# Second mixer: a head's two decay projections by seven block products, with token sums, weight sums and remainders on GpSimd

## The chip, the cores and the metric

The kernel runs on one core of one Trainium2 chip. The metric is the device time of one execution in microseconds (us); less is better. Engines are named as the profile names them: PE is TensorE, with PEld for its weight loads, DVE is VectorE, ACT is ScalarE, POOL is GpSimd and SP is SyncE, which issues most of the transfers.

## What is computed

Two layers of a diffusion backbone over 512 latent tokens with a prefix of 256 context tokens, model width 1024, all in float32. Layer 0 is a mixer of gated linear attention beside grouped-query attention and then a feed-forward block; layer 1 is an HGRN2 mixer and a feed-forward block. The change touches layer 1's mixer alone. What that computes, cut to the parts that matter:

```python
q, f_fwd, f_bwd, i, og = split(h @ w_in)          # h: 768 tokens x 1024, eight heads of 128 columns each
q = silu(q)
for d, f in enumerate((f_fwd, f_bwd)):            # the two decay projections of a head
    log_f = logaddexp(log(lb[d]), log1p(-lb[d]) + log_sigmoid(f))
    k = -expm1(log_f)                             # that is (1 - lb) * (1 - sigmoid(f))
    o[d] = scan(q, k, i, log_f)                   # context first, from a zero state; then the latent tokens
out = rms(o[0] + o[1]) * gain * silu(og)          # latent tokens alone
```

The decay projections are needed for all 768 tokens, the query projection and the gate og for the 512 latent ones.

## The kernel before

A float32 product is made of three matmuls. Each operand is split into H, a copy in the format that TensorE multiplies at speed, and L = x - H, the remainder; the product is H·H + H·L + L·H (`mm3`, and `product` in the change). A weight block goes through `fetched` (L793): a transfer into a `raw` buffer of 128x1024 (three of them), a cast to `wH` on ACT (L803) and a subtraction into `wL` on DVE (L804); there are four `wH` and four `wL` buffers. The activations of the mixer, `h`, lie split in four tiles `x0` to `x3`: H and L of its first four row blocks of 128, and H and L of its last four, each over 768 tokens.

The feed-forward blocks already make their 256-column products in seven block products in place of eight (`seven`, L900, with the table `SEVEN` at L59): the 1024 rows are cut into two halves, the columns into two blocks of 128, the tokens into two halves of 384. Sums of token halves (T1 to T4) are multiplied with sums of weight blocks (U1, U2, S4, V), and DVE and ACT put the results together.

The second mixer, `odd_mixer` (L1400), goes through the heads in a software pipeline. `prep` makes a head's projections: for each direction d a 128-column block of weights against 256 context and 512 latent tokens (`gemm_T`, tile `ff`, L1414 to L1418), a sigmoid (L1419), the gates `f`, `fc`, `kc`, `arr` (L1423 to L1426), the running product over the context (L1431, L1436) and `kc` times it (L1439); then the query projection (`fq`, L1444) with q = silu, two products q·f and the sum `ks` (L1446 to L1450). After the `yield` it transposes `kc` (`kcT`) and makes the first states (`S0`). `scan` (L947) then runs on the head before: seven levels, each with two copies on ACT (L1012), two products arr·f in place on DVE (L1017) and one f·f (L1018); block matrices (`pch`, `pbh`), transposes (`knph`), states (`pdh`, L1084) and outputs (`poh`), whose rms needs a power on POOL (`rstd`, L686). The order of these pieces on PE is written out by the `go(...)` lines at the end of `odd_mixer`, and held to by `pinned`: PE's instructions run in the order of the text. The other engines' instructions are ordered by the framework's scheduler, and each engine runs its queue in order.

Ahead of the mixer the projection i of the scan is made (`values`, L2124, tile `nat`), while DVE adds up the modulation vectors of layer 1 (`mod_late`, L573, tile `macc`, L613 and L615); a few matmuls on those sums (`mod_acc`) stand among PE's `nat` matmuls, in the written order. Behind the mixer's heads come the gate products (`gate`, tile `nat`) and the output projection.

PSUM has eight banks: two double ones (`mm`), two `sc`, two `tr`. The `hg` pool holds the mixer's tiles and takes the place of pools that the feed-forward block has released; a tile waits for the last use of what lay there.

Of the kernel before, what the change touches and what calls it, by code (L numbers as in the profile page):

```python
# [8 lines left out]
F32 = mybir.dt.float32  # L9
F32R = mybir.dt.float32r  # L10
# [306 lines left out]
class Net:  # L317
# [24 lines left out]
    def banks(self, narrow):  # L342
        if self.ps is not None:
            self.ps.release()
        self.narrow = narrow
        self.ps = self.tc.alloc_tile_pool(name={True: "psn", False: "psw", None: "pso"}[narrow], bufs=1, space=PSUM, reuse_waits="tile")
# [21 lines left out]
    def sc_tile(self, name, which=None):  # L368
        if which is None:
            self.side = which = 1 - self.side  # L370
        return self.ps.tile([P, 512], F32, tag=f"sc{which}", bufs=1, name=name)

# [574 lines left out]
    def scan(self, pool, nm, arr, q, ksum, dscale, f, nt, hpp, V, first, ends, o_evac):  # L947
# [54 lines left out]
        while b < P:  # L1002
            qk = pool.tile([P, 2, N], F32, tag=f"qk{N}", bufs=4 if N > CTX else 3, name=f"qk{nm}{b}")
            qks[b] = qk

            blk = arr.rearrange("p a (n h o) -> p a n h o", h=2, o=b)
            qkv = qk.rearrange("p a (n h o) -> p a n h o", h=2, o=b)
            nb = N // (2 * b)
            tv = f[:, :, : 2 * nb].rearrange("p a (n h) -> p a n h", h=2)
            for lo, half in ((0, 0), (2, 1)):  # L1010
                dst = blk[:, lo : lo + 2, :, half, :]
                nc.scalar.copy(qkv[:, :, :, half, :], dst)  # L1012
                tb = tv[:, :, :, 1 - half]
                if lo == 2:
                    tb = tb[:, ::-1, :]
                tb = tb[:, :, :, None].to_broadcast([P, 2, nb, b])
                nc.vector.tensor_tensor(dst, dst, tb, op=ALU.mult)  # L1017
            nc.vector.tensor_tensor(f[:, :, :nb], tv[:, :, :, 0], tv[:, :, :, 1], op=ALU.mult)  # L1018
# [49 lines left out]
        for d, (order, steps) in enumerate(orders):  # L1068
# [10 lines left out]
            for i, t in enumerate(steps):  # L1079
                S = pool.tile([P, P], F32, tag="S", bufs=8 if hpp > 1 else 10, name=f"S{nm}{d}{t}")  # L1080
# [318 lines left out]

    def odd_mixer(self, h, fi):  # L1400
        nc, I = self.nc, self.I
        w = I["odd_w_in"][0]
        with self.pool("hg") as gp:
            ones = gp.tile([P, CTX], F32, tag="ones", name="ones")
            nc.gpsimd.memset(ones, 1.0)
            def prep(hd, given):
# [3 lines left out]
                ks = gp.tile([P, SEQ], F32, tag="ks", bufs=2, name=f"ks{hd}")  # L1410
                S0, kcs = [], []
                for d in range(2):
                    pt = self.mm_tile(f"ff{hd}{d}")
                    W = self.unit_cols(w, (1 + d) * D + hd * P)  # L1414
                    self.gemm_T(pt, W, h, ((512, 256),))
                    yield
                    self.gemm_T(pt, W, h, ((0, 512),))
                    sg = gp.tile([P, NT], F32, tag="sg", bufs=2, name="sg")  # L1418
                    nc.scalar.activation(sg, pt[:, :NT], AF.Sigmoid)  # L1419
                    lb, lb1, nlb1 = (x[:, d, hd : hd + 1] for x in (self.lb, self.lb1, self.nlb1))  # L1420
                    fc = gp.tile([P, CTX + 32], F32, tag="fc", bufs=2, name="fc")
                    kc = gp.tile([P, CTX], F32, tag="kc", bufs=2, name="kc")
                    nc.vector.tensor_scalar(fc[:, :CTX], sg[:, SEQ:], lb1, lb, op0=ALU.mult, op1=ALU.add)  # L1423
                    nc.scalar.activation(kc, sg[:, SEQ:], AF.Identity, bias=lb1, scale=nlb1)
                    nc.vector.tensor_scalar(f[:, d, :], sg[:, :SEQ], lb1, lb, op0=ALU.mult, op1=ALU.add)
                    nc.scalar.activation(arr[:, 2 * d, :], sg[:, :SEQ], AF.Identity, bias=lb1, scale=nlb1)  # L1426

                    pr = gp.tile([P, CTX], F32, tag="pr", bufs=1, name="pr")
                    if d == 0:
                        nc.vector.memset(pr[:, CTX - 1 : CTX], 1.0)  # L1430
                        nc.vector.tensor_tensor_scan(  # L1431
                            pr[:, 0 : CTX - 1][:, ::-1], fc[:, 1:CTX][:, ::-1], ones[:, 1:CTX], 1.0, op0=ALU.mult, op1=ALU.mult
                        )
                    else:
                        nc.vector.memset(pr[:, 0:1], 1.0)
                        nc.vector.tensor_tensor_scan(  # L1436
                            pr[:, 1:CTX], fc[:, 0 : CTX - 1], ones[:, 1:CTX], 1.0, op0=ALU.mult, op1=ALU.mult
                        )
                    nc.vector.tensor_tensor(kc, kc, pr, op=ALU.mult)  # L1439

                    kcs.append(kc)
                    yield
                pq = self.mm_tile(f"fq{hd}")
                self.gemm_T(pq, self.unit_cols(w, hd * P), h, ((0, 512),))  # L1444
                q = gp.tile([P, SEQ], F32, tag="q", bufs=2, name=f"q{hd}")
                nc.scalar.activation(q, pq[:, :SEQ], AF.Sigmoid)  # L1446
                nc.vector.tensor_tensor(q, q, pq[:, :SEQ], op=ALU.mult)
                nc.vector.tensor_tensor(arr[:, 1, :], q, f[:, 1, :], op=ALU.mult)
                nc.vector.tensor_tensor(arr[:, 3, :], q, f[:, 0, :], op=ALU.mult)
                nc.vector.tensor_tensor(ks, arr[:, 0, :], arr[:, 2, :], op=ALU.add)  # L1450
# [3 lines left out]
                for kc in kcs:  # L1454
                    pk = self.tr_tile("kcT")
                    for i in range(2):
                        self.tr(pk[:, i * P : (i + 1) * P], kc[:, i * P : (i + 1) * P], self.ident)
                    kn = gp.tile([P, CTX], F32, tag="kcn", bufs=2, name="kcn")
                    nc.scalar.copy(kn, pk[:, :CTX])
                    kns.append(kn)  # L1460
# [16 lines left out]
            def head(hd, arr, q, ks, f, S0):  # L1477
# [3 lines left out]
                def evac(hh, t0, n, po):  # L1481
                    o = fi[:, 0:LT, hd * P : (hd + 1) * P]
                    nc.scalar.copy(o, po)
                    sq = gp.tile([P, LT, P], F32, tag="sq", bufs=1, name="sq")
                    nc.scalar.activation(sq, po, AF.Square)
                    ss = self.sm.tile([P, LT], F32, tag="ss4", name="ss4")
                    nc.vector.tensor_reduce(ss, sq, axis=AX.X, op=ALU.add)
# [3 lines left out]
                return self.scan(gp, f"h{hd}", arr, q, ks, 1.0, f, LT, 1, V, S0, None, evac)  # L1491

            def gate(c0, early):
                us = self.wide_units(4 * D + c0)
                for t0 in (0, 2):
# [6 lines left out]
                    for a in range(2):  # L1502
                        pt = self.mm_tile("nat")[:, :512]
# [14 lines left out]
            for hd in range(8):  # L1518
# [4 lines left out]
                go(new, new)  # L1523
# [17 lines left out]

        cat = Split(h.pool)
# [742 lines left out]
```

## Time and profile before

| | before |
|---|---|
| median of 3 runs | 1674.42 us (1673.77 to 1677.1) |
| the profiled execution | 1675.78 us, its span 1674.0 us |
| TensorE clock granted, mean | 0.998 |
| DVE busy, whole span | 1311.1 us, 78% |
| ACT busy, whole span | 916.1 us, 55% |
| POOL busy, whole span | 129.4 us, 8% |
| the eight heads' projections on PE | from 982.0 to 1221.1 us |

A row of a group gives line, engine, operation, output<-inputs, the shape and the count; then the busy time in us and the mean of one in ns; then how long the engine was idle just before, and what ended that. A row of the timeline gives start and duration in us. A row of the chain gives start, duration and what ran. A row of the windows gives the stretch, its length and the busy time of PE, PEld, DVE, ACT and POOL with the number of instructions. A row of merged instructions (x2, x3) spans from the first start to the last end.

### The profile page before, as it was taken

The page shows a single profiled execution, that of the slowest core. Times are in us where ns is not written, and L with a number is a line of the kernel's source. Part 1 is how long each engine was busy: PE and PEld are TensorE (multiplying, and loading weights), DVE is VectorE, ACT ScalarE, POOL GpSimd, SP SyncE. Part 2 cuts the span into 40 slices and gives each one's busy share as a digit, 9 for nine tenths or more (in the row PEclk, how much of TensorE's full clock was granted, in tenths as well). Part 3 has the DMA queues.
Part 4 walks back from the last instruction along what each step waited for, and adds up shares of the span by engine and source line. Part 5 has one row for each costly group of instructions (what it writes and reads, how often), then busy time and mean ns, then how long its engine had stood idle before and what let it go on. Part 6 is the DMA issues. An engine that isn't in the chain of part 4 may idle for free.

```text
span 1674.0 us, 32524 instructions
## 1 busy us (share of the span) xinstructions
PE 1644.8 (98%) x13407; PEld 1481.1 (88%) x13407; DVE 1311.1 (78%) x2097; ACT 916.1 (55%) x1551; POOL 129.4 (8%) x139
## 2 busy tenths in 40 slices
PE   9999999999999999999999999999999999999998
PEld 7899987888999999998887888888888899999886
DVE  5999678976898988777668648788775599987887
ACT  5745567845544443446447436666664565555664
POOL 2004110011000000002102000000000100000310
PEclk9999999999999999999999999999999999999999
DMA  9641012164243445249525541121124333333973
GB/s 336 213 132 41 3 45 86 50 227 160 80 126 114 139 151 176 78 153 205 100 84 193 200 127 57 48 65 40 51 65 150 126 114 115 114 101 102 226 164 138
DMA packets 184736, 204.79 MB, mean 122 GB/s; under 512 B 7142, under 2 KB 141836, under 8 KB 184588
## 3 DMA queue, kind: packets, MB, share of 16 engines
q1 hardware_dynamic: 173996, 181.98, 34.7%
q0 software_dynamic: 9024, 17.30, 5.9%
q10 hardware_dynamic: 1568, 3.43, 0.6%
q8 instruction: 105, 1.72, 0.4%
q14 instruction: 43, 0.35, 0.1%
HBM read 193.23 MB, written 9.46 MB: 121 GB/s over the span
## 4 chain that ended last, share of the span: by engine, by line
PE 83%; DVE 8%; ACT 3%; DMA 3%; issue 2%; POOL 0%; SPq 0%; DVEq 0%; ACTq 0%; POOLq 0%
PE nat L355 12%; PE a L355 10%; PE ff L355 8%; PE E L355 7%; PE oproj L355 6%; PE x L355 6%; PE o L355 5%; PE D L355 4%; PE b L355 3%; PE fq L355 3%; PE gqk L355 2%; PE pearly L355 2%; PE q L355 2%; PE S L355 2%; PE poh L355 1%
## 5 line engine op out<-in xcount | busy, mean ns | idle before, releaser
L355 PE MATMUL nat<-wH,x 128*128 128x256 f32 (+2 forms) x968 | 226.7, 322 | 1.2 <-ACT x L2014 0.6
L860 ACT CAST wH<-raw 128x1024 fp32r<-128x1024 f32 x120 | 124.8, 1051 | 102.7 <-DVE raw L885 40.7
L355 PEld LDWEIGHTS nat<-wH,x 128*128 128x128 f32 x968 | 161.9, 190 | 19.5 <-ACT natq L1196 1.7
L861 DVE TENSOR_TENSOR wL<-raw,wH 128x1024 fp32r<-128x1024 f32 x120 | 145.7, 1222 | 23.6 <-ACT wH L860 23.3
L355 PE MATMUL nat<-wL,x 128*128 128x256 f32 (+2 forms) x484 | 153.5, 317 | 1.8 <-DVE wL L804 1.8
L804 DVE TENSOR_TENSOR wL<-raw,wH 128x1024 fp32r<-128x1024 f32 x79 | 95.8, 1222 | 50.6 <-ACT wH L803 49.8
L355 PE MATMUL ff<-x,wH 128*128 128x512 f32 (+1 forms) x512 | 127.6, 340 | 0.0
L686 POOL TENSOR_TENSOR rs<-ms,neghalf 128x1 f32<-128x1 f32 (+2 forms) x56 | 60.1, 1076 | 777.7 <-DVE ms L684 777.6
L803 ACT CAST wH<-raw 128x1024 fp32r<-128x1024 f32 x79 | 82.2, 1050 | 68.5 <-PE ff L355 19.7
L355 PE MATMUL oproj<-wH,x 128*128 128x512 f32 x320 | 102.2, 394 | 0.4 <-ACT x L1330 0.4
L355 PEld LDWEIGHTS nat<-wL,x 128*128 128x128 f32 x484 | 92.1, 190 | 7.8 <-DVE wL L804 2.7
L615 DVE SCALAR_TENSOR_TENSOR macc<-mraw,scT,macc 128x1024 f32<-128x1024 f32 x70 | 88.0, 1282 | 11.6 <-DMA mraw<-in_mod_w_dram 11.4
L355 PEld LDWEIGHTS ff<-x,wH 128*128 128x128 f32 x512 | 87.3, 190 | 10.0
L355 PE MATMUL x<-wH,two 128*128 128x512 f32 x280 | 90.5, 392 | 0.9 <-DVE y L1851 0.7
L1773 POOL DMA_DIRECT2D t<-in_ffn_w_down_dram x36 | 41.9, 1200 | 640.1 <-DVE t L1812 338.3
L1012 ACT COPY qkh<-arr 128x512 f32<-128x512 f32 x112 | 70.2, 641 | 36.6 <-DVE arr L1017 32.3
L355 PE MATMUL ff<-x,wL 128*128 128x256 f32 (+1 forms) x256 | 86.2, 337 | 0.0
L885 DVE TENSOR_TENSOR raw<-raw 128x512 f32<-128x512 f32 x120 | 82.8, 690 | 2.8
L1017 DVE TENSOR_TENSOR arr<-arr,f 128x512 f32<-128x512 f32 x112 | 74.4, 688 | 2.0 <-ACT qkh L1012 0.3
L355 PEld LDWEIGHTS oproj<-wH,x 128*128 128x128 f32 x320 | 59.9, 188 | 13.0 <-ACT x L1330 1.0
L355 PE MATMUL a<-T,wH 128*128 128x384 f32 (+1 forms) x320 | 70.5, 309 | 0.6 <-ACT qb L923 0.5
L355 PE MATMUL E<-T,wH 128*128 128x384 f32 (+1 forms) x320 | 70.4, 309 | 0.7 <-DVE go L938 0.7
(425 smaller groups left out, 4558.6 us busy)
## 6 DMA issues: line engine op xcount, KB each, us to landing
mraw<-in_mod_w_dram SPq DMA_DIRECT2D x80, 512.0 KB, 4.4
raw<-in_ffn_w_gate_dram SPq DMA_DIRECT2D x44, 512.0 KB, 3.9
raw<-in_ffn_w_up_dram SPq DMA_DIRECT2D x44, 512.0 KB, 4.9
raw<-in_odd_w_in_dram SPq DMA_DIRECT2D x40, 512.0 KB, 3.7
t<-in_ffn_w_down_dram POOLq DMA_DIRECT2D x30, 512.0 KB, 8.3
raw<-in_ffn_w_down_dram SPq DMA_DIRECT2D x28, 512.0 KB, 8.0
mraw<-in_mod_w_dram SPq DMA_DIRECT2D x32, 256.0 KB, 6.3
raw<-in_even_w_in_dram SPq DMA_DIRECT2D x16, 512.0 KB, 5.9
```

The costliest lines, as they stand in the source:

```text
L355: return self.pin(self.nc.tensor.matmul(*a, **k))
L615: nc.vector.scalar_tensor_tensor(a, u, w, a, op0=ALU.mult, op1=ALU.add)
L686: nc.gpsimd.tensor_tensor(rs, ms, self.neghalf.to_broadcast([P, w]), op=ALU.pow)
L803: self.casts = self.casts[-1:] + [nc.scalar.copy(H[:, :m], raw[:, :m])]
L804: vector.tensor_tensor(L[:, :m], raw[:, :m], H[:, :m].bitcast(F32), op=ALU.subtract)
L860: self.nc.scalar.copy(H, f)
L861: self.nc.vector.tensor_tensor(L, f, H.bitcast(F32), op=ALU.subtract)
L885: add = lambda o, x, y: nc.vector.tensor_tensor(o, x, y, op=ALU.add)
L1012: nc.scalar.copy(qkv[:, :, :, half, :], dst)
L1017: nc.vector.tensor_tensor(dst, dst, tb, op=ALU.mult)
L1773: add = lambda o, src: self.pin(nc.gpsimd.dma_start(out=o, in_=src, accum_op=ALU.add))
```

## The change

- **Products.** A head's two directions become the two column blocks of one product of 1024 rows, 256 columns and 768 tokens, cut as in `SEVEN`: 7 products of 4 row blocks x 3 matmuls with 384 columns, in the order 11, 22, U1, 12, U2, S4, V. Before there were 2 x 8 x 3 matmuls with 256 columns and as many with 512. ACT copies or negates four results out of PSUM, DVE adds four more; the sigmoid is taken in three pieces.
- **Token sums.** `half_sums`, traced ahead of the first head, makes T1, T2, T4 and T3 (128x1536 each, H and L, in a new pool `T` of 48 KB a partition): 13 two-input operations on POOL, with four casts on ACT and four subtractions on DVE. The sums are used by all eight heads.
- **Weights.** A head's two decay blocks come in two transfers as before (and a third for the query). POOL makes the sums in place (four additions of 128x512); each of nine operands of 128x512 gets its H from ACT and its remainder L from POOL, in a ring of four places cut out of two of the four `wH` and `wL` buffers. The other two become four places for the scan's levels (`qk`), which lose their own tiles.
- **Smaller moves.** `ks` is added on POOL; `q` and `ks` lie in an `mraw` buffer; the running product is made in place, without `fc`, `pr` and `ones`; the squares of the outputs stay in PSUM, where DVE sums them; the S ring has 8 places in place of 10.
- **PSUM.** Four single banks `p0` to `p3` take the place of the two double ones in the mixer; A and D change banks from head to head.
- **Order.** `prep` has six steps in place of seven: products 11 and 22; U1, 12 and U2; S4 and V; the query; the transposes; the first states. One `go(new, new)` becomes `go(new)`.
- **Gate.** The first gate block's weights go into the places of T1, T2, T4 and T3.

```diff
+    def half_sums(self, h, pool, temp):
...
+        a, b = (temp().rearrange("p a n -> p (a n)")[:, : 4 * n].rearrange("p (k n) -> p k n", k=4) for _ in range(2))
+        op = lambda o, x, y, f: nc.gpsimd.tensor_tensor(o, x, y, op=f)
...
+            if sign > 0:
+                nc.scalar.copy(H, x)
+                nc.vector.tensor_tensor(L, x, H.bitcast(F32), op=ALU.subtract)
...
+        def less(x, y):
+            op(a, f32[x][0], f32[y][0], ALU.subtract)
+            op(b, f32[x][1], f32[y][1], ALU.subtract)
+            op(a, a, b, ALU.add)
+
+        less("11", "12")
+        split("T1", a)
+        for i in range(2):
+            op(b if not i else b, a if not i else b, f32["22"][i], ALU.add)
+        split("T2", b, -1.0)
+        for i in range(2):
+            op(a, b if not i else a, f32["21"][i], ALU.subtract)
+        split("T4", a)
+        less("22", "12")
+        split("T3", a)
...
+            def operand(x):
+
+                H, L = turned(ring)
+                nc.scalar.copy(H, x)
+                nc.gpsimd.tensor_tensor(L, x, H.bitcast(F32), op=ALU.subtract)
+                return [z.rearrange("p (k n) -> p k n", k=4) for z in (H, L)]
+
+            def weights(hd):
+                (w11, w12), (w21, w22) = (fetch((1 + d) * D + hd * P) for d in range(2))
+                add = lambda o, x, y: nc.gpsimd.tensor_tensor(o, x, y, op=ALU.add)
+                yield operand(w11)
+                yield operand(w22)
+                add(w22, w21, w22)
+                yield operand(w22)
+                yield operand(w12)
+                add(w21, w21, w11)
+                add(w11, w11, w22)
+                yield operand(w11)
+                add(w12, w12, w11)
+                yield operand(w12)
+                yield operand(w21)
+
+            def product(pt, W, X, start, stop):
+                for k in range(4):
+                    for i, (x, y) in enumerate(((0, 0), (0, 1), (1, 0))):
...
-                for d in range(2):
-                    pt = self.mm_tile(f"ff{hd}{d}")
-                    W = self.unit_cols(w, (1 + d) * D + hd * P)
-                    self.gemm_T(pt, W, h, ((512, 256),))
-                    yield
-                    self.gemm_T(pt, W, h, ((0, 512),))
...
+                    product(pt, next(W), forms[xn], new, True)
...
+                nc.gpsimd.tensor_tensor(ks, arr[:, 0, :], arr[:, 2, :], op=ALU.add)
...
-                nc.vector.tensor_tensor(ks, arr[:, 0, :], arr[:, 2, :], op=ALU.add)
...
                 go(outs, old)
-                go(new, new)
+                go(new)
                 go(outs, old, scan)
                 go(new, new)
                 go(scan, scan)
```

More of the change, by code (lines that the diff above doesn't have):

```diff
@@ L1402, in odd_mixer, with turned, fetch @@
         w = I["odd_w_in"][0]
+        n2 = NT // 2
+        tp = self.open_pool("T")
         with self.pool("hg") as gp:
[L1404 to L1405 removed]
+            self.banks(4)
+            own = {x: [self.wp.tile([P, WU], F32R if i < 2 else F32, tag=f"w{x}", bufs=4, name=f"w{x}") for i in range(4)] for x in "HL"}
+            ring = [[own[x][i // 2][:, 512 * (i % 2) : 512 * (i % 2) + 512] for x in "HL"] for i in range(4)]
+            levels = [own[x][i].rearrange("p (a n) -> p a n", a=2) for i in (2, 3) for x in "HL"]
+            forms = self.half_sums(h, tp, lambda: gp.tile([P, 4, SEQ], F32, tag="arr", bufs=2, name="Tsum"))
+            ones = self.one.to_broadcast([P, CTX - 1])
+            order = [SEVEN[i] for i in (0, 4, 1, 2, 3, 5, 6)]
+            def turned(xs):
+                x = xs.pop(0)
+                xs.append(x)
+                return x
+            def fetch(c0):
+                r = self.wp.tile([P, WU], F32, tag="raw", bufs=3, name="raw")
+                nc.sync.dma_start(out=r.rearrange("p (k n) -> p k n", k=KD), in_=w[:, c0 : c0 + P].rearrange("(k p) m -> p k m", p=P))
+                return [r[:, 512 * i : 512 * i + 512] for i in range(2)]
+            def operand(x):
[20 more added lines that the diff above has]
+                    for i, (x, y) in enumerate(((0, 0), (0, 1), (1, 0))):
+                        self.mm(
+                            pt, W[x][:, k, :], X[y][:, k, :], start=start and k == 0 and i == 0, stop=stop and k == 3 and i == 2,
+                            skip_group_check=True,
+                        )
```

134 lines of the change are left out of this document (90 added, 44 removed).

## The prediction

> **What bounds the kernel now.** I read the page's busy shares first, then the chain of work that ended last, then one head's stretch of it.
>
> ```profile
> PE 1644.8 (98%) x13407; PEld 1481.1 (88%) x13407; DVE 1311.1 (78%) x2097; ACT 916.1 (55%) x1551; POOL 129.4 (8%) x139
> ...
> PE 83%; DVE 8%; ACT 3%; DMA 3%; issue 2%; POOL 0%; SPq 0%; DVEq 0%; ACTq 0%; POOLq 0%
> ```
>
> PE is the bound overall. The change sits in layer 1's mixer, so that stage decides. The chain there, and the busy times of the stretch from one head's `ff` piece to the next head's:
>
> ```profile
> 448.52 2.08 PE E L355 x12
> ...
> 982.29 16.68 PE ff L355 x96
> ...
> 1081.27 5.68 PE ff L355 x24
> 1086.95 5.44 PE fq L355 x24
> ...
> 1094.97 2.88 PE ff L355 x24
> ...
> 1099.62 8.35 PE ff L355 x48
> ```
>
> ```profile
> 1081.27:1112.80 31.53, 31.53 (x400) 28.10 (x399) 25.12 (x57) 19.68 (x36) 1.44 (x1) 1.00 0.18 52
> ```
>
> A head takes 31.53 us, PE is busy in all of it, and the granted clock is full. DVE has 25.12 us of work, ACT 19.68, POOL 1.44. Only PE's work sets the pace; DVE has 6.4 us to spare.
>
> **PE's saving.** A head's `ff` pieces are 5.68 + 2.88 + 8.35 = 16.91 us. A block product of the new shape (12 matmuls of 384 columns) exists in the feed-forward block: 2.08 us. Seven make 14.56. So 2.35 us go per head and the head would take 29.18; the first head's piece (16.68) loses 2.1. Seven heads and the first: 7 x 2.35 + 2.1 = **-18.6 us**, if nothing else makes PE wait. All else of PE stays.
>
> **DVE per head.**
>
> ```profile
> L1017 DVE TENSOR_TENSOR arr<-arr,f 128x512 f32<-128x512 f32 x14 | 9.3, 687 | 0.1
> L804 DVE TENSOR_TENSOR wL<-raw,wH 128x1024 fp32r<-128x1024 f32 x3 | 3.7, 1225 | 1.7 <-ACT wH L803 1.7
> L1018 DVE TENSOR_TENSOR f<-f 128x32 f32<-128x32 f32 (+6 forms) x7 | 2.2, 307 | 0.1
> ...
> L1439 DVE TENSOR_TENSOR kc<-kc,pr 128x256 f32<-128x256 f32 x2 | 0.8, 422 | 0.1
> ...
> L1489 DVE TENSOR_TENSOR fi<-fi,rs 128x512 f32<-128x512 f32 x1 | 0.7, 692 | 0.9 <-POOL rs L686 0.9
> ...
> L1448 DVE TENSOR_TENSOR arr<-q,f 128x512 f32<-128x512 f32 x1 | 0.7, 686 | 0.0
> ...
> L1431 DVE TENSOR_TENSOR_SCAN pr<-fc,ones 128x255 f32<-128x255 f32 x1 | 0.7, 683 | 0.0
> ...
> L1450 DVE TENSOR_TENSOR ks<-arr 128x512 f32<-128x512 f32 x1 | 0.7, 665 | 0.0
> ```
>
> ```profile
> L931 DVE TENSOR_TENSOR go<-go,b 128x384 f32<-128x384 f32 x10 | 5.5, 551 | 0.5 <-PE b L355 0.3
> ```
>
> DVE loses the three remainders (3.7) and `ks` (0.7) and gains four additions out of PSUM of 0.55 (2.2): 25.1 - 4.4 + 2.2 = 22.9, with the two dropped memsets 22.8. Of that, operations with two inputs in SBUF are 9.3 + 2.2 + 0.8 + 0.7 + 2 x 0.7 (q·f) + 2 x 0.7 (running products) = 15.8 us, or 69%.
>
> **ACT per head.**
>
> ```profile
> L803 ACT CAST wH<-raw 128x1024 fp32r<-128x1024 f32 x3 | 3.1, 1048 | 3.0 <-PE fq L355 1.9 <-PE ff L355 1.1
> ```
>
> ```profile
> L860 ACT CAST dH<-ws 128x512 fp32r<-128x512 f32 x40 | 24.9, 621 | 28.1 <-PE a L355 17.4 <-DVE ws L885 10.7
> L923 ACT COPY go<-a 128x384 f32<-128x384 f32 x10 | 4.8, 481 | 29.7 <-DVE zy L1735 19.0 <-PE E L355 7.3 <-DVE qb L1735 3.0
> ```
>
> Three casts go (3.1); nine of 0.62 come (5.6), and four copies of 0.48 (1.9). Cutting the sigmoid costs little; I estimate 0.2 from the shapes. 19.7 + 4.6 = 24.3 of 29.18: fuller, not the bound.
>
> **POOL per head.** It gets nine remainders, four weight sums and `ks`: 14 operations of 128x512.
>
> ```profile
> L804 POOL TENSOR_TENSOR wL<-zraw,wH 128x576 fp32r<-128x576 f32 x4 | 5.7, 1417 | 22.7 <-ACT wH L803 22.7
> L686 POOL TENSOR_TENSOR rs<-ms,neghalf 128x4 f32<-128x4 f32 x6 | 8.5, 1409 | 224.1 <-DVE ms L684 224.1
> ```
>
> ```profile
> 168.43 1.04 POOL L1382 TENSOR_TENSOR natq<-natq,rs 128x512 f32<-128x512 f32 x1
> 169.43 0.45 POOL L1382 TENSOR_TENSOR natk<-natk,rs 128x128 f32<-128x128 f32 x1
> ```
>
> The 512-wide one with a broadcast operand took 1.04 us, the 128-wide 0.45, which leaves some 0.25 fixed. The remainder with two full operands took 1.417 at 576 columns; scaled, 0.25 + 1.167 x 512/576 = 1.29. I take 1.28, nearest in kind; the ends are 1.04 and 1.42. 14 x 1.28 + 1.4 for the power = 19.3 us of 29.18. POOL's own time would be hidden. The new waits: each remainder waits in POOL's queue for ACT's cast, each cast for a free place of the four, that is for the product four back on PE; behind a waiting remainder stand the power (DVE's `fi` waits for it) and `ks` (PE's `pch` waits for it, some 15 us later in the order). With PE's pieces other than products, about 13 us per head, POOL has time to refill the four.
>
> **What POOL does to DVE** decides the sign. The trace has POOL operations beside DVE:
>
> ```profile
> 126.82 1.04 POOL L1382 TENSOR_TENSOR natq<-natq,rs 128x512 f32<-128x512 f32 x1
> ...
> 162.01 1.29 POOL L1382 TENSOR_TENSOR natq<-natq,rs 128x512 f32<-128x512 f32 x1 [7.29 <-DVE natq L1381]
> ```
>
> ```profile
> 127.04 1.10 DVE L1017 TENSOR_TENSOR arrg<-arrg,glaf 128x256 f32<-128x256 f32 x1
> ...
> 135.33 0.75 DVE L1017 TENSOR_TENSOR arrg<-arrg,glaf 128x256 f32<-128x256 f32 x2
> ...
> 162.32 1.26 DVE L1017 TENSOR_TENSOR arrg<-arrg,glaf 128x256 f32<-128x256 f32 x1
> ```
>
> Two such DVE operations take 0.75 alone, so one about 0.41; under POOL's `natq` it took 1.10 and 1.26. One POOL operation of 1.04 held DVE up by 0.69 and 0.85. Scaled to 1.28 that is 0.85 to 1.05; I take 0.95. If it strikes a two-input operation 69% of the time, the 14 cost DVE 14 x 0.95 x 0.69 = 9.2 us, and DVE needs 22.8 + 9.2 = 32.0 us per head where PE needs 29.18. Then **DVE is the bound**. Its queue runs in order, so waits add: `fi` already waits 0.9 us on POOL's power, which will stand behind a remainder. I take 32.5 per head: (32.5 - 31.53) x 8 = **+8 us** in place of -18.6. Ends: no hold-up, 29.18 (-18.6); each of the 14 at 1.05, 37.5 (+48).
>
> The Trainium skill, "SBUF — State Buffer", "Who interferes with whom", says that a DVE instruction with two SBUF inputs and a GpSimd one that reads SBUF exclude each other for the whole instruction, and counts fp32 copies and tensor_scalars among DVE's as well. The full 1.28 for each would make it 22.8 + 14 x 1.28 x 0.69 = 35.2 us per head, an estimate; the rows above, 0.69 and 0.85 of 1.04, stay under it.
>
> **The token sums.** Thirteen POOL operations of 128x1536 can begin when the last activations of `x0` and `x1` are in, and stand in POOL's queue ahead of the first weights.
>
> ```profile
> 933.91 0.69 DVE L764 TENSOR_TENSOR x<-hf,x 128x512 fp32r<-128x512 f32 x1 [1.13 <-ACT x L763]
> ...
> 971.48 1.28 DVE L615 SCALAR_TENSOR_TENSOR macc<-mraw,scT,macc 128x1024 f32<-128x1024 f32 x1 [0.81 <-DMA mraw<-in_mod_w_dram]
> ```
>
> ```profile
> 973.95 0.99 PE mod_acc L355 x8
> ```
>
> ```profile
> 976.64 0.32 POOL L1405 MEMSET ones<- 128x256 f32 x1 [52.34 <-PE nat L355]
> ```
>
> ```profile
> L615 DVE SCALAR_TENSOR_TENSOR macc<-mraw,scT,macc 128x1024 f32<-128x1024 f32 x14 | 17.8, 1284 | 8.0 <-DMA mraw<-in_mod_w_dram 7.9
> L804 DVE TENSOR_TENSOR wL<-raw,wH 128x1024 fp32r<-128x1024 f32 x6 | 7.2, 1222 | 5.3 <-ACT wH L803 5.2
> L764 DVE TENSOR_TENSOR x<-hf,x 128x512 fp32r<-128x512 f32 x3 | 2.1, 692 | 3.4 <-ACT x L763 3.4
> ```
>
> ```profile
> L98 DVE TENSOR_TENSOR T<-f,T 128x1536 fp32r<-128x1536 f32 x2 | 3.5, 1755 | 0.0
> ```
>
> The sums start at 933.91 + 0.69 = 934.6, when POOL has nothing else. `ones`, the pool's first tile, waited until 976.64 for a `nat` operand; T3 takes that place now and is written last, so I expect no wait there. One of 1536 takes between 0.25 + 3 x 0.79 = 2.6 (broadcast slope) and 0.25 + 1.167 x 1536/576 = 3.4; I take 3.3, by the full-operand row. T4, the second product's operand, is ready after seven of them, 23 us, at 958 at best, well before 982. Undisturbed, all 13 end about 978, and the start costs some 3 us (remainders behind them).
>
> But from 934.6 to 982 DVE has two-input work of its own: 17.8 + 2.1 + four weight remainders (3 of the 6 stay, and `wx`; 4 x 1.22 = 4.9) + the remainders of T1, T2 and T4 (3 x 1.755 = 5.3) = 30 us. Ten sums, less 0.25 each, are 30.5. In turn that is 60 us in a stretch of 47.4: 13 late. T3 (3 x 3.05 + 1.755 = 11) and the first head's 11 weight operations (11 x 1.05 = 11.5) then fall on 14.56 us of products: 8 more. PE stands in written order behind `mod_acc`, whose last sum ended at 972.76, 1.2 us ahead of it, so DVE's delay reaches PE at once. I take **+20 us**; ends 0 and +35.
>
> ```profile
> raw<-in_odd_w_in_dram SPq DMA_DIRECT2D x40, 512.0 KB, 3.7
> ```
>
> Transfers stay three per head, on SP's queue, 3.7 us to landing, with a head's time of lead; PSUM's new banks and the gate's new places I cost at nothing, hidden by PE's `fq` (5.44 us); uncovered, one cast and remainder, 2.3 us, once.
>
> **The sum.** 1675.78 + 8 + 20 = 1703.8 for an execution like the profiled one, which lies 1.36 above the median of 1674.42; so **1702**.
>
> **Rivals.** *Faster* (0.28): POOL's operations fall into DVE's 6.4 us of idle and 7 us of other operations. It decides as soon as one costs DVE under (29.18 - 22.8)/14 = 0.46 us on average and the start under 18.6. For it: POOL can run ahead of PE by four operands, and T's are wanted late. Against: 0.69 and 0.85 measured. Time: 1674.4 - 18.6 + 3 = 1659 (1655 to 1670). *Only the start suffers* (0.17): heads at 29.2 to 30.3, start +20: 1676 to 1686. *Every operation holds DVE up* (0.07): heads at 34 and more, 1720 to 1745. *The sums do not start early* (0.04): if they wait as `ones` did, until 976.6, T4 comes 23 + 4 us later and PE idles some 20: 1690 to 1715. My forecast has 0.44, 1686 to 1720.
>
> **Range and chances.** 1659 to 1718 leaves out the worst case, half of the fast one's lower part and the forecast's top: under 0.2. The likeliest case alone is 1686 to 1720. Faster by over 0.2% (about what a measurement of this kernel can tell from no change) is the first rival, 0.28; within 0.2%, 1671 to 1678, the low end of the second, 0.06; slower 0.66.
>
> **What would show it.** Right: DVE's L1017 mean well above 687 ns, DVE busy near 100% of a head's stretch, PE waiting on `arr`, `CTh` or `wL`, `macc` ending after 985. Wrong: L1017 still near 690, PE busy in the whole head at 29.2. The PE term is checked by the new products at 2.08 us each. It would also be wrong if POOL's 512-wide operations took far from 1.28, or the sums began late.

## The result and the profile after

| | before | after |
|---|---|---|
| median of 4 runs each, on one chip | 1674.1 us (1673.67 to 1677.1) | 1754.2 us (1753.69 to 1756.07) |
| ratio, 95% interval | | 1.0476 (1.0458 to 1.0495) |
| span of the profiled execution | 1674.0 us | 1752.3 us |

The change costs 80 us where 28 were predicted. The profile's page after it: the busy shares, the chain of work that ended last by engine, and the group of the products arr·f.

```profile
PE 1654.6 (94%) x13311; PEld 1498.5 (86%) x13311; DVE 1400.5 (80%) x2085; ACT 946.9 (54%) x1643; POOL 335.8 (19%) x260
...
PE 70%; DVE 18%; ACT 4%; issue 3%; DMA 2%; POOL 2%; DVEq 0%; SPq 0%; ACTq 0%; POOLq 0%
...
L1020 DVE TENSOR_TENSOR arr<-arr,f 128x512 f32<-128x512 f32 x112 | 96.7, 892 | 2.0
```

Before, DVE had 8% of the chain and one arr·f took 687 ns; now it has 18%, and the same operation takes 892. Where the time lies is read from a landmark that both kernels have, the `pch` matmuls that read `q` and `ks`: the first of them, in the first head, and the last, in the last head (the tile's view; first and last start). The first row is of before, the second of after:

```profile
L355 PE MATMUL pch<-q,ks x256: 196/196/217, 1016.9 to 1237.6; 128*32 128x32 f32 x128
```

```profile
L355 PE MATMUL pch<-qks x256: 196/196/218, 1044.5 to 1314.8; 128*32 128x32 f32 x128
```

The first head reaches it 27.6 us later. From the first to the last it is 270.3 in place of 220.7 us: +49.6, at 38.6 us for a steady head where 31.53 stood. Behind the last 1.1 are lost. These three make the spans' difference of 78.3. So there are two places to explain, the heads and the start.

One head after, from the windows, and in it DVE's groups, GpSimd's groups and PE's waits:

```profile
1203.11:1241.69 38.58, 31.91 (x394) 29.90 (x396) 34.29 (x54) 22.77 (x47) 21.29 (x16) 0.91 0.15 43
```

```profile
L1020 DVE TENSOR_TENSOR arr<-arr,f 128x512 f32<-128x512 f32 x14 | 12.2, 900 | 0.2
L1021 DVE TENSOR_TENSOR f<-f 128x32 f32<-128x32 f32 (+6 forms) x7 | 5.6, 803 | 0.1
L1524 DVE TENSOR_TENSOR_SCAN sg<-sg,one 128x255 f32<-128x255 f32 x2 | 2.9, 1468 | 0.0
L1520 DVE TENSOR_SCALAR sg<-sg,lb,lb 128x256 f32<-128x256 f32 x2 | 2.3, 1142 | 0.1
...
L1600 DVE TENSOR_REDUCE ss<-poh 128x4 f32<-128x512 f32 x1 | 0.7, 691 | 2.5 <-ACT poh L1598 2.5
L1602 DVE TENSOR_TENSOR fi<-fi,rs 128x512 f32<-128x512 f32 x1 | 0.7, 691 | 1.1 <-POOL rs L689 1.1
...
L1552 DVE TENSOR_TENSOR sg<-sg,ffA 128x384 f32<-128x384 f32 x1 | 0.5, 544 | 0.0
```

```profile
L1472 POOL TENSOR_TENSOR wL<-raw,wH 128x512 fp32r<-128x512 f32 x10 | 14.4, 1445 | 16.5 <-ACT wH L1471 16.5
```

```profile
PE pdh L355 <- DVE CTh L1000: 6.1, 1, 6.1
```

PE has 31.91 us of work in 38.58 and stands 6.1 us waiting for one thing of DVE's. DVE has 34.29 us of work and stands for the other 4.29, in waits of its own order: DVE is the bound. The f·f products (f<-f, L1021) went from 307 to 803 ns, the running products from 683 to 1468. The reduction out of PSUM (691), and the additions with an input in PSUM (544; 551 in another block before) kept their lengths. So something strikes DVE's instructions among those that read from SBUF alone. The timeline of the same head shows what stands beside them; the first row is GpSimd's, the others are DVE's:

```profile
1213.28 4.40 POOL L1477 TENSOR_TENSOR raw<-raw 128x512 f32<-128x512 f32 x3
```

```profile
1213.67 1.50 DVE L1517 TENSOR_SCALAR f<-sg,lb,lb 128x512 f32<-128x512 f32 x1
1215.09 1.24 DVE L1021 TENSOR_TENSOR f<-f 128x8 f32<-128x8 f32 x1
1216.25 0.54 DVE L1552 TENSOR_TENSOR sg<-sg,ffA 128x384 f32<-128x384 f32 x1
1216.72 1.11 DVE L1520 TENSOR_SCALAR sg<-sg,lb,lb 128x256 f32<-128x256 f32 x1
...
1219.90 0.54 DVE L1517 TENSOR_SCALAR f<-sg,lb,lb 128x512 f32<-128x512 f32 x1
```

Beside GpSimd's three additions, `f` takes 1.50 us where the same operation takes 0.54 a little later, f·f 1.24 (0.17 before) and `fc` 1.11 (0.41 before); the addition with an input in PSUM, which runs wholly beside them, keeps its 0.54. In this head 13 of GpSimd's 14 operations fall on a DVE instruction in this way: ten on one with two inputs, 9.0 us longer together, and three on a tensor_scalar (`f` and `fc`, one input and two constants), 2.4 us. Less these 11.4 DVE's work is 22.9. GpSimd's remainders are long too, 1445 ns. The granted clock of 0.91 isn't the reason: PE waits.

### The profile page after: what moved, and what is told of

Same layout as the page of the kernel before. It is cut to its first block, busy times and chain, and to the rows that moved or that the text cites. A ratio compares the mean times of both kernels' runs of the same rounds, so it can differ in the third digit from the quotient of the medians.

```text
span 1752.3 us, 32612 instructions
## 1 busy us (share of the span) xinstructions
PE 1654.6 (94%) x13311; PEld 1498.5 (86%) x13311; DVE 1400.5 (80%) x2085; ACT 946.9 (54%) x1643; POOL 335.8 (19%) x260
## 4 chain that ended last, share of the span: by engine, by line
PE 70%; DVE 18%; ACT 4%; issue 3%; DMA 2%; POOL 2%; DVEq 0%; SPq 0%; ACTq 0%; POOLq 0%
PE a L355 11%; PE nat L355 10%; PE E L355 7%; PE x L355 6%; PE oproj L355 6%; PE o L355 5%; DVE arr L1020 4%; PE D L355 4%; PE b L355 4%; PE gqk L355 2%; PE pearly L355 2%; PE q L355 2%; PE S L355 1%; DVE f L1021 1%; PE attO L355 1%
## 5 line engine op out<-in xcount | busy, mean ns | idle before, releaser
L355 PE MATMUL nat<-wH,x 128*128 128x256 f32 (+2 forms) x904 | 206.2, 317 | 1.2 <-ACT x L2130 0.6
L863 ACT CAST wH<-raw 128x1024 fp32r<-128x1024 f32 x120 | 124.9, 1051 | 103.0 <-DVE raw L888 37.9
L864 DVE TENSOR_TENSOR wL<-raw,wH 128x1024 fp32r<-128x1024 f32 x120 | 145.6, 1220 | 23.7 <-ACT wH L863 23.2
L355 PE MATMUL nat<-wL,x 128*128 128x256 f32 (+2 forms) x452 | 141.0, 312 | 1.8 <-DVE wL L807 1.8
L1472 POOL TENSOR_TENSOR wL<-raw,wH 128x512 fp32r<-128x512 f32 x72 | 109.7, 1530 | 132.2 <-ACT wH L1471 116.9
L1020 DVE TENSOR_TENSOR arr<-arr,f 128x512 f32<-128x512 f32 x112 | 96.7, 892 | 2.0
L807 DVE TENSOR_TENSOR wL<-raw,wH 128x1024 fp32r<-128x1024 f32 x51 | 61.5, 1220 | 18.9 <-ACT wH L806 18.3
L355 PE MATMUL E<-x,wH 128*128 128x384 f32 (+1 forms) x320 | 70.7, 310 | 0.0
L355 PE MATMUL b<-x,wH 128*128 128x384 f32 (+1 forms) x320 | 70.6, 310 | 0.0
L355 PE MATMUL a<-b,wH 128*128 128x384 f32 (+1 forms) x320 | 70.4, 309 | 0.0
L355 PE MATMUL a<-x,dH 128*128 128x384 f32 (+1 forms) x320 | 70.3, 309 | 0.0
```

What stands on the lines that cost most here:

```text
L355: return self.pin(self.nc.tensor.matmul(*a, **k))
L807: vector.tensor_tensor(L[:, :m], raw[:, :m], H[:, :m].bitcast(F32), op=ALU.subtract)
L863: self.nc.scalar.copy(H, f)
L864: self.nc.vector.tensor_tensor(L, f, H.bitcast(F32), op=ALU.subtract)
L1472: nc.gpsimd.tensor_tensor(L, x, H.bitcast(F32), op=ALU.subtract)
```

## The experiments

**Theory**: GpSimd's and DVE's instructions hold each other up, which makes DVE the bound. **Rival A**: GpSimd's results come late, and PE waits for low halves. **Rival B**: DVE's written order, or ACT, is the bound by itself. For the start: the sums of the tokens, by their delay or by what they hold up. Runs without an interval below are single executions beside one of the kernel before on the same chip (1674 to 1675 us).

### Without GpSimd's work in the heads

`heads_without`:

```diff
+                if hd:
+                    L = forms["T3"][1].rearrange("p k n -> p (k n)")[:, :512]
+                else:
+                    nc.gpsimd.tensor_tensor(L, x, H.bitcast(F32), op=ALU.subtract)
...
-                add = lambda o, x, y: nc.gpsimd.tensor_tensor(o, x, y, op=ALU.add)
+                add = lambda o, x, y: None if hd else nc.gpsimd.tensor_tensor(o, x, y, op=ALU.add)
```

> The changed kernel, in heads 1 to 7 without GpSimd's nine remainders and four weight sums: the casts read the weights as they came, and PE multiplies by a fixed low half (that part of the computation is left out). GpSimd keeps ks and the power. Hold-up theory (GpSimd's and VectorE's instructions with operands in SBUF exclude each other, and VectorE is the bound in the heads): a head falls from 38.6 to 29.2 to 31 us, the 128x512 arr x f from 0.90 to 0.69 us, the whole to 1690 to 1702 us. Rival A (GpSimd's results come late and PE waits for low halves): the heads fall just as far, since the results aren't waited for. Rival B (VectorE's queue in its written order, or ScalarE, is the bound by itself): a head stays at 34 us or more, the whole above 1722 us.

`heads_unread` keeps all 13 operations, and gives PE the fixed low half after them:

```diff
                 nc.gpsimd.tensor_tensor(L, x, H.bitcast(F32), op=ALU.subtract)
+                if hd:
+                    L = forms["T3"][1].rearrange("p k n -> p (k n)")[:, :512]
...
-                add = lambda o, x, y: nc.gpsimd.tensor_tensor(o, x, y, op=ALU.add)
+                add = lambda o, x, y: nc.gpsimd.tensor_tensor(ring[0][1] if hd else o, x, y, op=ALU.add)
```

> As heads_without, but GpSimd does all of its 13 operations per head on the same inputs; what it writes is read by nobody in heads 1 to 7, and PE multiplies by the fixed low half. Hold-up theory: heads at 36 to 38.6 us, the whole 1738 to 1754 us, arr x f at 0.85 to 0.90 us. Rival A (late results): as heads_without, a head at 31 us at most, the whole under 1702 us. Rival B: as heads_without, wherever that lies.

Measured: 1693.1 us without, 1757.0 with the unread ones. A head's windows, first without, then with:

```profile
1101.90:1131.40 29.50, 29.50 (x387) 27.97 (x386) 23.51 (x54) 22.64 (x46) 2.31 (x2) 1.00 0.20 56
```

```profile
1125.80:1165.10 39.30, 31.92 (x410) 29.62 (x400) 34.37 (x54) 22.67 (x46) 21.52 (x15) 0.96 0.15 42
```

Without them PE is busy in all of the head, at full clock, and the head takes 29.5 us. With them, though nobody reads what they write, it takes 39.3, and DVE's busy time alone rises from 23.51 to 34.37. Rival A falls, for no result was waited for; rival B falls as a cause, for the same order with the same ACT work runs at PE's pace. What PE waits for in that head is DVE's, `CTh` for 5.2 us, `sg` for 1.3 and `Sh` for 0.9. Thirteen operations cost DVE 10.86 us, 0.84 each.

`heads_five` leaves five of the thirteen in, with the fixed low half for PE as before:

```diff
-                nc.gpsimd.tensor_tensor(L, x, H.bitcast(F32), op=ALU.subtract)
+                count[0] += 1
+                if not hd or count[0] % 9 in (0, 2, 4, 6, 8):
+                    nc.gpsimd.tensor_tensor(L, x, H.bitcast(F32), op=ALU.subtract)
```

> As heads_unread, with five of the nine remainders per head by GpSimd and none of the weight sums, five of thirteen operations (that part of the computation is left out). Price theory: heads_unread has 39.35 us and GpSimd's operations cost VectorE (34.4 - 23.5)/13 = 0.84 us each, beside 4.3 us in which it waits in its order; 23.5 + 4.3 + 5 x 0.84 = 32.0 us per head, the whole 1707 to 1715 us. If VectorE's waits fill up first: 29.5 to 31 us, 1693 to 1703 us. If a few operations are enough to upset the order: above 34 us.

Measured: 1709.0 us, 31.72 us per head. A head's windows, and in it all that DVE waited for:

```profile
1110.00:1141.72 31.72, 29.97 (x388) 27.96 (x387) 26.82 (x54) 22.75 (x45) 9.62 (x8) 1.00 0.18 51
```

```profile
DVE ss L1606 <- ACT poh L1604: 2.4, 1, 2.4
DVE fi L1608 <- POOL rs L689: 1.1, 1, 1.1
DVE sg L1526 <- ACT kc L1525: 0.7, 1, 0.7
```

It came out where a price per operation put it, though the price isn't flat: the five, all of them remainders, cost DVE 0.66 each (26.82 - 23.51), the other eight, four remainders and the four sums, 0.94 (34.37 - 26.82). Why the eight cost more was not tested. DVE is the bound with 26.8 us of work in 31.7, for PE, with 29.97 us of work, waits for `Sh` and `CTh` alone: it also stands 4.9 us in its own order, mostly in the turn from the states through PE's `poh` and ACT's squares back to `ss` and then `fi`. The same remainder is 4.3 in the changed kernel and 4.9 in `heads_unread`. With 29.5 for PE, 4.9 of waits and 23.5 of work, some 1.1 us were free by estimate: no more than two operations of GpSimd's at 0.66.

### GpSimd's work alone, in the kernel before

To see the hold-up without any other part of the change, 14 operations per head were put into the kernel before, written to a scratch tile that nobody reads: `before_with_adds`.

```diff
+            def idle(W, m):
+                x, y = (z.rearrange("p k n -> p (k n)")[:, :512].bitcast(F32) for z in W)
+                for _ in range(m):
+                    nc.gpsimd.tensor_tensor(scr[:, :512], x, y, op=ALU.add)
...
                     W = self.unit_cols(w, (1 + d) * D + hd * P)
+                    idle(W, 5)
```

> The kernel before, with 14 GpSimd additions of 128x512 per head put in (five behind each direction's weights, four behind the query's); they read wH and wL, write a scratch tile and nobody waits for them. Nothing else is changed, so PE's order, the products and the start are those of before. Hold-up theory: each costs VectorE some 0.8 us; 25.1 + 11.2 = 36.3 us of work per head in place of 31.53 of the pace, the heads at 36 to 39 us, the whole 1710 to 1735 us, arr x f above 0.85 us. Rival (the changed kernel is slower by its new products, PSUM banks and order, and GpSimd only takes part in them): within 3 us of 1674.

`before_with_memsets` and `before_with_copies` have another operation there, a memset of 128x1536 (the five or four of a block stand behind one addition of 128x8) and a copy of 128x512:

```diff
-                    nc.gpsimd.tensor_tensor(scr[:, :512], x, y, op=ALU.add)
+                    nc.gpsimd.memset(scr, 1.0)
...
-                    nc.gpsimd.tensor_tensor(scr[:, :512], x, y, op=ALU.add)
+                    nc.gpsimd.tensor_copy(scr, x)
```

> As before_with_adds, but in place of each addition a memset of 128x1536, which reads nothing, paced by one addition of 128x8 behind each block of weights. If GpSimd holds VectorE up by the operands it reads: within 4 us of 1674, arr x f at 0.69 us. If it does so by running or by writing at all: as with the additions, above 1700 us.

> As before_with_adds, with a copy of 128x512 (one input read) in place of each addition. If any read of SBUF by GpSimd holds VectorE up for the length of GpSimd's instruction: the heads above 33 us, the whole 1685 to 1735 us by the length of a copy. If only the second input does: within 4 us of 1674.

Measured: 1740.1, 1684.3 and 1679.9 us. A head of each, in that order:

```profile
1113.80:1154.10 40.30, 34.16 (x403) 30.40 (x404) 37.55 (x57) 19.43 (x36) 21.95 (x17) 0.92 0.15 44
```

```profile
1083.30:1116.00 32.70, 31.78 (x403) 28.18 (x405) 27.39 (x57) 19.44 (x36) 21.59 (x19) 1.00 0.17 51
```

```profile
1050.40:1082.50 32.10, 31.76 (x400) 28.16 (x398) 29.29 (x56) 19.70 (x35) 13.89 (x15) 1.00 0.18 51
```

The additions alone make the untouched kernel 65 us slower, 5 more than the worst end of what was expected: the first of its heads takes 54 us, the next five 37.8 to 40.4, and the last, where no more weights are made, 31.4. In the head shown DVE's work is 37.55 in place of 25.12. Over the five heads (1075.1 to 1271.0) it is 178.38 us where before has 125.64, with 63 additions: 0.84 each, the price of `heads_unread`. The copies cost it (29.29 - 25.12) / 14 = 0.30 each; memsets, busy as long as the additions (21.59 against 21.95), at most 0.16. So it is GpSimd's reading that holds DVE's two-input operations up. A copy, with one input, costs less than an addition, but it is also shorter, and the two were not told apart. The last two runs came out between the cases named for them: copies do cost DVE something, though less than it had idle, and the memsets' 9 us have another cause, read from the trace and not tested alone. It shows in DVE's groups of that head of memsets:

```profile
L1017 DVE TENSOR_TENSOR arr<-arr,f 128x512 f32<-128x512 f32 x14 | 9.3, 686 | 0.1
...
L1052 DVE COPY STh<-CTh 32x128 f32<-32x128 f32 x4 | 3.2, 810 | 0.0
...
L1500 DVE TENSOR_TENSOR fi<-fi,rs 128x512 f32<-128x512 f32 x1 | 0.7, 694 | 4.0 <-POOL rs L686 4.0
```

arr·f is untouched, while the copies `STh`, 216 ns in the kernel before, take 810, and `fi` waits 4.0 us since the power stands behind memsets in GpSimd's queue.

### The heads' work on DVE

`heads_dve` gives the nine remainders, four sums and `ks` to DVE, `no_gpsimd` the sums of the tokens too:

```diff
-                nc.gpsimd.tensor_tensor(L, x, H.bitcast(F32), op=ALU.subtract)
+                nc.vector.tensor_tensor(L, x, H.bitcast(F32), op=ALU.subtract)
...
-        op = lambda o, x, y, f: nc.gpsimd.tensor_tensor(o, x, y, op=f)
+        op = lambda o, x, y, f: nc.vector.tensor_tensor(o, x, y, op=f)
```

> The changed kernel with the nine remainders, four weight sums and ks of every head done by VectorE in place of GpSimd. VectorE's own work is then 22.8 + 14 x 0.67 = 32.2 us per head. Hold-up theory: a head takes 32.5 to 34.5 us, since adding 9.4 us to VectorE costs less than what GpSimd holds it up; the whole 1705 to 1725 us, faster than the changed kernel's 1754. Rival A (late results): VectorE's queue runs these in order, so latency stays; a head at 33 us or more, not told apart here. Rival B: VectorE gets 9.4 us more on top of what bounds it now: 1754 us or more.

> As heads_dve, and the 13 sums of the tokens by VectorE too (about 1.75 us each, 22.8 us). Hold-up theory for the start: VectorE's 30 us and these 22.8 no longer exclude another engine, 53 us in a stretch of 48, so the start loses some 8 to 12 us of its 28 in place of all: the whole 1704 to 1714 us where heads_dve had 1724. Queue theory for the start (in heads_dve the sums stop for 40 us, since T1's cast waits in ScalarE's queue behind weight casts that wait for places held by the last nat products): who adds does not matter, the first pch stays 20 us or more late, the whole 1718 us or more.

Measured: 1724.4 and 1713.1 us, some 35 us per head in both. DVE doing the work itself is 30 us faster than GpSimd doing it, 4.7 of them at the start: 0.68 for a remainder on DVE against 0.84 for the same one on GpSimd, without counting GpSimd's own 1.45. It is still slower than before, with 30.72 us of work and 4.2 of waits in a head, which at 35.0 us is a little over the 34.5 expected. `no_gpsimd` gains at the start, where its first `pch` comes 13.5 us earlier than that of `heads_dve`, as the first theory of its expectation had it. (There are ten sums of the tokens; "13" in the expectation repeats a miscount of the prediction.)

Could the waits be taken away? `rms_scalar` puts the squares' sums, with ACT's accumulator, and the scaling of `fi` on ACT; `rms_gates_scalar` also f, fc and the copies `STh`; `all_moved` has the latter with the token sums of the next section.

```diff
-                    nc.vector.tensor_reduce(ss, po, axis=AX.X, op=ALU.add)
...
+                        nc.scalar.activation(po[:, t, :], po[:, t, :], AF.Square, accum_out=ss[:, t : t + 1])
...
+                        nc.scalar.mul(o[:, t, :], o[:, t, :], rs[:, t : t + 1])
```

> As no_gpsimd, with a head's rms off VectorE: the squares' sums by ScalarE's accumulator, the small scaling by GpSimd, the multiplication by ScalarE. A head there takes 34.7 us with 30.7 us of work on VectorE, which waits 2.9 us for the squares and 1.1 for the power. If VectorE's in-order waits are the rest of its bound: work 29.2 us and no such wait, the heads at 30 to 31.5 us, the whole 1685 to 1695 us. Rival (the heads without GpSimd are bound by ScalarE's queue or PE's order): 33.5 us or more, the whole above 1703 us.

> As rms_scalar, and the four tensor_scalars of f and fc and the four copies of STh by ScalarE too, 2.8 us of VectorE's work per head. VectorE is then at 26.4 us, under PE's 29.2; ScalarE at 28 or so. If VectorE's work was the bound: the heads at 29.4 to 30.5 us, the whole 1676 to 1688 us. Rival (ScalarE, now nearly full, is the next bound): 31.5 us or more, no better than rms_scalar.

> As rms_gates_scalar, but with the sums of the tokens and the casts of T1 to T4 by GpSimd as in sums_cast_there. If both theories hold: heads at 29.4 to 30.5 us and the first pch under 10 us late, the whole 1668 to 1682 us, level with the kernel before or a little faster. If ScalarE bounds the heads: 1685 us or more.

In all three the theory named first fell, with 1729.8, 1720.1 and 1738.95 us (all_moved: ratio to before 1.0386, 1.0368 to 1.0403; its start missed too, with the first `pch` 28.7 us late). A steady head takes 37.5 us in the last two. These heads lie where the rivals put them, but ACT is not full as the last two rivals had it, with 28.0 us of work in 37.5; and `rms_gates_scalar` is 9.7 us faster than `rms_scalar`, where its rival had no gain. In a head of `rms_scalar` the windows, what DVE waits for and what PE waits for:

```profile
1142.00:1179.70 37.70, 32.11 (x377) 29.42 (x369) 29.35 (x65) 24.73 (x56) 1.20 (x2) 0.91 0.17 45
```

```profile
DVE arr L1020 <- ACT wL L1015: 4.3, 1, 4.3
DVE sg L1539 <- PE ffB L355: 1.9, 1, 1.9
```

```profile
PE ffE L355 <- DVE wL L1472: 3.3, 1, 3.3
```

DVE has 1.4 us less work and 4 more of waits: the turn through `poh` now stands in ACT's queue, and the levels' copies, for which DVE's arr·f waits, stand behind it. No engine is full in this head: PE 32.1, DVE 29.4, ACT 24.7 of 37.7. What the next bound is was not settled; that in this order moving the wait to ACT didn't pay is shown. No version here beats the kernel before.

### The start

`no_sums` lets the products read plain blocks in place of T1 to T4 and leaves out the sums.

```diff
+        forms.update(T1=forms["11"], T2=forms["22"], T3=forms["21"], T4=forms["12"])
```

> The changed kernel without the sums of the tokens: the products take the plain blocks 11, 22, 21 and 12 in place of T1 to T4 (the sums and their splits are left out). Heads as before the edit. Sums theory: the start's 28 us up to the first pch go nearly whole, the whole 1726 us (1722 to 1732). Rival (the start is late by the first head's small casts and remainders, eleven on GpSimd, or by the mod sums on VectorE): 1740 to 1754 us.

Measured: 1723.9 us, and the first `pch` at 1014.8: the sums cost 29.7 us, and without them the first head is 2.1 ahead of before. The chain of waits of the changed kernel from 975.99 on:

```profile
975.99 2.48 DVE macc L618 x2
978.51 1.92 PE mod_acc L355 x4
980.43 3.65 PE nat L355 x12
984.16 0.63 ACT wH L1471
984.86 1.29 POOL wL L1472
986.15 3.40 POOL Tsum L1416
989.56 2.74 POOL wL L1472
...
1014.84 3.50 POOL Tsum L1416
1018.36 0.75 ACT T L1421
```

and some of GpSimd's instructions there:

```profile
949.47 2.29 POOL L1472 TENSOR_TENSOR wL<-raw,wH 128x512 fp32r<-128x512 f32 x1 [25.48 <-ACT wH L1471]
...
961.65 8.92 POOL L1416 TENSOR_TENSOR Tsum<-x 128x1536 f32<-128x1536 f32 x2
970.66 4.33 POOL L1416 TENSOR_TENSOR Tsum<-Tsum 128x1536 f32<-128x1536 f32 x1
984.86 1.29 POOL L1472 TENSOR_TENSOR wL<-raw,wH 128x512 fp32r<-128x512 f32 x1 [9.88 <-ACT wH L1471]
```

The last activations are in at 938. In GpSimd's queue two remainders and three weight sums stand ahead of them, and the first of these waits for its weights until 949. After three sums a remainder waits 9.9 us for a cast whose place in the ring one of PE's last `nat` products still holds. The chain then runs on GpSimd from 984.86 to 1018.3.

Two experiments asked whether the delay is in the products' wait for T or in a queue. `sums_unread` makes all sums, and the products read the plain blocks; `sums_cast_there` is `heads_dve` with the casts of T1 to T4 on GpSimd:

```diff
+            forms = dict(made, T1=made["11"], T2=made["22"], T3=made["21"], T4=made["12"])
```

```diff
-                nc.scalar.copy(H, x)
+                nc.gpsimd.tensor_copy(H, x)
...
-                nc.scalar.mul(H, x, -1.0)
+                nc.gpsimd.tensor_scalar(H, x, -1.0, None, op0=ALU.mult)
```

> The changed kernel with all token sums and their splits made as there, but the products take the plain blocks 11, 22, 21 and 12, so nobody waits for T1 to T4 in the heads (that leaves the sums out of the products). The changed kernel's start is 29.7 us behind no_sums. Late-sums theory: its PE waits 12.1 us for T4 and 5.2 for gc, which stands behind T1's remainder on VectorE; without the wait for T the first pch comes 12 to 20 us earlier, the whole 1734 to 1742 us. Rival (the sums cost by holding VectorE up, ahead of the heads and in the first): at most 8 us earlier, 1746 us or more.

> As heads_dve (the heads' remainders, weight sums and ks on VectorE, the ten sums of the tokens on GpSimd), with the four casts of T1 to T4 by GpSimd too, behind the sums. Queue theory for the start (the sums stop for 40 us in heads_dve, since T1's cast stands in ScalarE's queue behind weight casts that wait for places held by the last nat products): the sums run on from 933 without a stop, the first pch comes within 10 us of 1016.9 in place of 22.9 later, the whole 1708 to 1714 us. Rival (the sums hold VectorE's mod sums up, wherever their casts are): the mod sums end later still, the first pch 18 us or more late, the whole 1718 us or more.

Measured: 1757.5 and 1731.4 us. In both, the theory named first in the expectation fell. In `sums_unread` nobody reads T, and the first `pch` comes at 1048.9, no earlier: T3's cast on ACT waits 11.25 us for its sum, and in ACT's queue the sigmoids stand behind it. In `sums_cast_there` the sums begin at 933, but after five of them GpSimd stops for 37 us. The next sum needs the place that T1's remainder reads, and that remainder stands in DVE's queue behind the mod sums and two weight remainders, until 995.69. And the early five hold DVE up where PE needs it. The rows are GpSimd's, DVE's and PE's wait:

```profile
997.53 6.94 POOL L1416 TENSOR_TENSOR Tsum<-Tsum,x 128x1536 f32<-128x1536 f32 x2 [37.39 <-DVE modcol L502]
```

```profile
995.69 1.75 DVE L1422 TENSOR_TENSOR T<-Tsum,T 128x1536 fp32r<-128x1536 f32 x1
```

```profile
PE nat L355 <- DVE wL L807: 8.9, 1, 8.9
```

Five kernels with different orders agree in one thing, by the end of the last sum and the first `pch` behind it:

| | last sum ends | first pch | between |
|---|---|---|---|
| after | 1018.3 | 1044.5 | 26.2 |
| sums_unread | 1022.4 | 1048.9 | 26.5 |
| sums_cast_there | 1020.4 | 1046.5 | 26.1 |
| heads_dve | 1014.4 | 1039.8 | 25.4 |
| no_gpsimd | 999.0 | 1026.3 | 27.3 |

Where GpSimd makes the sums, the first four rows, the first head's sigmoids stand behind T3's cast in ACT's queue or wait for what stands behind T3's remainder in DVE's. There the last sum sets the start, whoever reads it. In `no_gpsimd` the chain runs through T4's remainder (992.83) and PE's products instead, so its 27.3 is no proof of this. An order that gets the sums done early and holds nothing up was not tried.

## Why the prediction was wrong

For an execution like the profiled one 1703.8 us were forecast and 1754.07 came. Of these 50.3 us 41.6 lie in the heads (+8 taken, +49.6 measured), 7.6 at the start and 1.1 behind the heads.

- **PE's saving** held. The prediction had 29.18 us for a head and 2.1 saved in the first; where nothing makes PE wait, `heads_without` has 29.5, and `no_sums` is 2.1 ahead.
- **DVE as the bound, held up by GpSimd**: the mechanism was right, and so was DVE's own work (22.8 taken; 22.9 is left of the 34.29 in the head shown when the 11.4 of lengthening are taken off).
- **The hold-up was mis-sized**: 9.2 us per head taken, 11.4 measured in the head shown. The step "it strikes a two-input operation 69% of the time" failed in what it leaves out. Ten of the 14 operations do strike one, 71%, and cost 9.0 us. Three more strike a tensor_scalar, which the prediction put at nothing, and cost 2.4: fc takes 1142 ns on average, where it takes 409 in `heads_dve`. The Trainium skill, "SBUF — State Buffer", "Who interferes with whom", counts these among the struck; this trace agrees, and the 35.2 that the prediction worked out by that section is nearer DVE's 34.3 than the 32.0 it took, by luck in part: it takes 1.28 for a strike, where 0.88 is the average of the 13, and leaves the tensor_scalars out.
- **DVE's waits were the larger miss**: the prediction went from 32.0 to 32.5, half a microsecond, and named only `fi` behind the power. Measured are 4.3: 2.45 for the squares, 1.13 for the power and the rest small. The trace before had this wait for the squares already, 3.3 us in every head (the row stands below this list), and the prediction put it at nothing without a reason. 2.3 of work and 3.8 of waits make the 6.1 us by which a head is longer than forecast. With these waits DVE becomes the bound at some 25 us of work, by estimate. The threshold of the faster rival, 0.46 us per operation, left them out: with 14 operations at any price measured for two inputs, that rival was out.
- **The token sums**: +20 taken, +27.6 measured, inside its ends of 0 and 35, by another path. "Thirteen operations" was a miscount: the change has ten. They do not "stand in POOL's queue ahead of the first weights"; five weight operations stand ahead of them, and they begin at 961.65, not at 934.6. PE waited 3.7 us for `mod_acc`, not 13. What decides is GpSimd's queue up to the tenth sum. The 13 came from the miscount: T1, T2 and T4 take seven sums, not ten, and 30 + 7 x 3.05 = 51.4 us in 47.4 are 4 late, which would have made the +20 some +12. That +20 lay as near as it did is luck. The rival in which the sums do not start early was given 0.04.
- **The end** was costed at nothing and cost 1.1.
- **The range** ended at 1718. "Every operation holds DVE up", 1720 to 1745, is the rival that came in the heads, with 34 us and more, and was given 0.07; no case joined it with a late start.

DVE's wait for the squares before, in the stretch from 1081.27 to 1112.80, which touches two of them:

```profile
DVE ss L1487 <- ACT sq L1485: 6.5, 2, 3.3
```

## What to carry to other kernels

Before work is given to GpSimd, read DVE's spare time as the period less its work and less those of its in-order waits that stay when DVE is the bound; in `heads_without` 6.0 us of idle were 1.1 of spare by estimate. A GpSimd operation with two inputs in SBUF costs DVE as much as doing it there, or more: here 0.66 us each with five in a head and 0.84 with thirteen, against 0.68. Operations moved to a queue start when the one ahead of them can, so read what stands ahead of them and what it waits for.

## What the hardware showed unexpectedly

- When a GpSimd addition strikes, DVE's two-input operation gets up to 1.1 us longer: in `before_with_adds` running products take 1752 ns and one q·f 1755, where they take 683 and 686 alone.
- A GpSimd copy of 128x512 takes 897 ns on average beside DVE (`before_with_copies`) and costs DVE 0.30; an addition takes 1456 beside DVE (median, `before_with_adds`) and costs 0.84.
- A memset of 128x1536 on GpSimd (1415 ns) leaves arr·f at 686 ns, but makes DVE's copies of 32x128 take 810 in place of 216. The Trainium skill, "SBUF — State Buffer", "Who interferes with whom", says both: a two-input instruction of DVE contends with GpSimd's reads alone, and copies take the shared ports in their two-port mode.
